# 24 weight tiles get their low half from an accumulating DMA instead of a GpSimd subtraction

## The chip, the cores and the metric

The kernel runs on one core of one Trainium2 chip. A core has five instruction queues that work side by side, each in its own order: TensorE (PE, matrix products; PEld is its weight load), VectorE (DVE), ScalarE (ACT), GpSimd (POOL) and SyncE (SP, which only issues DMAs). They wait for each other by semaphores. The time is device microseconds of one launch: median 2107.94 us of three runs (2106.41 to 2108.83).

## The reference

A residual stream of 256 tokens by 2048 channels in float32 goes through two layers, an S5 state-space mixer and windowed attention, each followed by a squared-ReLU MLP. The change lies in the gated unit at the end of the S5 mixer:

```python
    y = lax.map(per_example, ug).reshape(bsz, seq, dm)
    y = y + d_skip.astype(f32) * uf
    z = jax.nn.gelu(y).astype(u.dtype)
    return (z @ w_glu_a) * jax.nn.sigmoid(z @ w_glu_b)
```

`y` is the output of a bidirectional scan over time. Both weight matrices are 2048 by 2048 float32.

## The kernel before

**Products in three parts.** To get float32 accuracy, each weight tile is split into a high half in the format fp32r and a low half, raw minus high, also in fp32r. `mm3` (L686 to L688) makes each product in three matmuls: activation high times weight high (L686), activation low times weight high (L687), activation high times weight low (L688). So a tile's first two matmuls need only its high half, the third its low half.

**Preparing a tile.** `wload` takes the next tile from the list `self.wsrc`: it issues the load from HBM into a raw buffer (L662), casts it into the high half on ScalarE (L667) and subtracts into the low half (L668), on VectorE or, where the table `self.whow` says "g", on GpSimd. `wnext` calls `wload` ahead of use, one tile ahead as a rule. Buffers go round in rings that `wring` sets up: two raw buffers, three for high halves, three for low halves. For the early tiles of the gated unit two more raw buffers are lent (`wx`), until the eight output blocks of the second half begin and the third of them is done.

**The early gated unit.** Its weights come in 32 early tiles of 128 by 1024 (512 KB, `wge`), each loaded by a DMA that *ScalarE* issues, and 16 later tiles of 128 by 2048 (1 MB, `wgl`), loaded by SyncE. Each early tile feeds twelve matmuls of 128x512. The early tiles (`glu_early`, run by `glu` in `run`) depend only on the first half of `z`, so they are put between the pieces of the S5 mixer's second half: the scan on VectorE (L532 to L534), the expansion of the kernels on GpSimd (L550, L551) with their matmuls (L572) and copies out of PSUM (L590), and then eight output blocks, each with state copies (L608), matmuls (L636), every second one with a gelu (L641), a transposition (L648) and its split (L651, L652). Tiles 9 to 32 are the ones that the range `WP` marks (L1271): their subtraction is GpSimd's. Behind them come the 16 `wgl` tiles and then the MLP.

**What sets the order.** The program is written in one order and then rearranged by a scheduler at build time, so the order in each queue is what the listings of the instructions show. On the chip each queue keeps that order strictly: an instruction that waits holds back all that stand behind it on its engine, a DMA issue on ScalarE or GpSimd too.

Of the kernel before, what the change touches and what calls it, by code (L numbers as in the profile page):

```python
# [9 lines left out]
F32 = mybir.dt.float32  # L10
# [3 lines left out]
ALU = mybir.AluOpType  # L14
# [21 lines left out]
WP = range(9, 33)  # L36
# [131 lines left out]
class Kernel:  # L168
# [486 lines left out]
    def wload(self):  # L655
        if self.wsrc:
            src = self.wsrc.pop(0)
            if src is None:
                self.wring(D)
                src = self.wsrc.pop(0)  # L660
            raw, hi, lo = (r.next() for r in self.wr)
            (self.nc.scalar if raw.shape[1] < D else self.nc.sync).dma_start(raw, src)  # L662
            how = self.whow.get(len(self.wsrc), "v")
            m = raw.shape[1] // len(how)
            for i, e in enumerate(how):
                c = slice(i * m, (i + 1) * m)
                self.nc.scalar.copy(hi[:, c], raw[:, c])  # L667
                (self.nc.gpsimd if e == "g" else self.nc.vector).tensor_sub(lo[:, c], raw[:, c], hi[:, c].bitcast(F32))  # L668
            self.wq.append((hi, lo))

# [505 lines left out]
    def run(self):  # L1176
        nc, d, ar = self.nc, self.d, self.ar
# [8 lines left out]
        v, g = nc.vector, nc.gpsimd  # L1186
# [78 lines left out]
        def glu(n, m=GM):  # L1265
            for _ in range(n):
                next(ge, None)
                sc(m)

        n = len(self.wsrc)  # L1270
        self.whow.update({n - i: "g" for i in WP})  # L1271
        glu(GO)
        self.s5_ztrans(0, prev)
        ar.free("st0", "u0")
# [2 lines left out]
        raw = self.wr[0].tiles  # L1277
# [120 lines left out]
```

## Time and profile before

| | before |
|---|---|
| median of three runs | 2107.94 us |
| span of the profiled execution, first to last instruction | 2103.6 us |
| what the median has beyond that span | 4.3 us |
| instructions | 33054 |
| GpSimd busy in the whole span | 331.0 us |
| of it the subtractions L668 (all 36) | 101.1 us |
| wait of TensorE for L668 of GpSimd (matmuls) | 8.1 us in 5 waits, the longest 4.0 us |

The profile has a page of one execution: busy time per engine, the span in slices, the DMA queues, the chain that ended last, and groups of instructions by line. The trace behind it answers further: a timeline (start, duration, engine, line, operation, output and inputs, count, and in brackets the idle time before with what ended it), busy time per stretch of the span, and waits. "slot" stands for any piece of the big on-chip buffer, "bank" for PSUM. The span is what one execution's instructions cover; the runs' times contain a few microseconds more.

The profiled execution has no run time of its own on record beside its span, so the table sets the span beside the median of the runs.

### The profile page before, as it was taken

The page shows a single profiled execution, that of the slowest core. Times are in us where ns is not written, and L with a number is a line of the kernel's source. Part 1 is how long each engine was busy: PE and PEld are TensorE (multiplying, and loading weights), DVE is VectorE, ACT ScalarE, POOL GpSimd, SP SyncE. Part 2 cuts the span into 40 slices and gives each one's busy share as a digit, 9 for nine tenths or more (in the row PEclk, how much of TensorE's full clock was granted, in tenths as well). Part 3 has the DMA queues.
Part 4 walks back from the last instruction along what each step waited for, and adds up shares of the span by engine and source line. Part 5 has one row for each costly group of instructions (what it writes and reads, how often), then busy time and mean ns, then how long its engine had stood idle before and what let it go on. Part 6 is the DMA issues. An engine that isn't in the chain of part 4 may idle for free.

```text
span 2103.6 us, 33054 instructions
## 1 busy us (share of the span) xinstructions
PE 2030.6 (97%) x13844; PEld 1705.0 (81%) x13844; DVE 1245.0 (59%) x1824; ACT 974.7 (46%) x1238; POOL 331.0 (16%) x248
## 2 busy tenths in 40 slices
PE   4989999999999999999999889999999999999999
PEld 4877778788888888888887667888888888888887
DVE  8889736655555554444556877465555555444444
ACT  6553645444444444434434556554444444443442
POOL 6988721200000000000003330100000000000000
PEclk9999999999999999999999999999999999999999
DMA  3224455455555555655554332455555555555554
GB/s 120 73 93 144 152 199 196 154 200 188 193 180 184 193 184 200 213 188 199 202 186 153 115 128 96 146 185 200 188 193 186 195 184 196 200 187 193 200 187 153
DMA packets 59685, 364.28 MB, mean 173 GB/s; under 512 B 6816, under 2 KB 9152, under 8 KB 19600
## 3 DMA queue, kind: packets, MB, share of 16 engines
q1 hardware_dynamic: 54144, 342.32, 46.4%
q10 hardware_dynamic: 5184, 19.49, 2.8%
q8 instruction: 108, 1.77, 0.3%
q0 software_dynamic: 208, 0.36, 0.0%
q14 instruction: 41, 0.34, 0.0%
HBM read 360.05 MB, written 2.10 MB: 172 GB/s over the span
## 4 chain that ended last, share of the span: by engine, by line
PE 75%; DVE 4%; ACT 2%; DMA 1%; issue 1%; POOL 0%; SPq 0%; ACTq 0%; DVEq 0%
PE bank L878 33%; PE bank L827 23%; PE bank L828 11%; PE bank L686 2%; PE bank L687 2%; PE bank L688 2%; DVE slot L668 1%; ACT slot L667 1%; ACT slot L1039 1%; PE bank L1058 1%; DMA slot<-in_wqkv 1%; PE bank L1049 1%; DVE slot L1043 1%; DVE slot L1024 1%; DMA slot<-in_wup 0%
## 5 line engine op out<-in xcount | busy, mean ns | idle before, releaser
L668 DVE TENSOR_TENSOR slot<-slot,slot 128x2048 fp32r<-128x2048 f32 (+1 forms) x321 | 713.6, 2225 | 737.0 <-ACT slot L667 733.3
L667 ACT CAST slot<-slot 128x2048 fp32r<-128x2048 f32 (+2 forms) x357 | 623.5, 1752 | 743.0 <-PE bank L878 368.4
L827 PE MATMUL bank<-slot,slot 128*128 128x512 f32 x2048 | 720.0, 397 | 0.0
L878 PE MATMUL bank<-slot,slot 128*128 128x512 f32 x3072 | 696.7, 389 | 0.0
L878 PEld LDWEIGHTS bank<-slot,slot 128*128 128x128 f32 x3072 | 576.5, 188 | 119.6
L828 PE MATMUL bank<-slot,slot 128*128 128x256 f32 x2048 | 572.0, 280 | 0.0
L827 PEld LDWEIGHTS bank<-slot,slot 128*128 128x128 f32 x2048 | 385.5, 188 | 92.5
L828 PEld LDWEIGHTS bank<-slot,slot 128*128 128x128 f32 x2048 | 386.9, 189 | 0.3
L686 PE MATMUL bank<-slot,slot 128*128 128x512 f32 x544 | 217.3, 401 | 6.8 <-ACT slot L667 5.2
L688 PE MATMUL bank<-slot,slot 128*128 128x512 f32 x544 | 207.7, 395 | 8.3 <-POOL slot L668 8.1
L687 PE MATMUL bank<-slot,slot 128*128 128x512 f32 x544 | 213.6, 393 | 0.0
L686 PEld LDWEIGHTS bank<-slot,slot 128*128 128x128 f32 x544 | 102.7, 189 | 31.4 <-ACT slot L667 6.5
L836 ACT ACTIVATE slot<-slot 128x256 f32<-128x256 f32 x128 | 53.6, 420 | 160.4 <-DVE slot L835 160.4
L688 PEld LDWEIGHTS bank<-slot,slot 128*128 128x128 f32 x544 | 101.6, 188 | 32.0 <-POOL slot L668 10.1
L687 PEld LDWEIGHTS bank<-slot,slot 128*128 128x128 f32 x544 | 102.8, 189 | 20.4 <-issue 0.5
L668 POOL TENSOR_TENSOR slot<-slot,slot 128x1024 fp32r<-128x1024 f32 (+2 forms) x36 | 101.1, 2818 | 102.5 <-ACT slot L667 97.2
L949 POOL DMA_DIRECT2D slot<-in_pos x1 | 0.8, 754 | 613.1 <-DVE slot L871 613.1
L532 DVE TENSOR_TENSOR bank<-bank,slot 128x256 f32<-128x256 f32 x126 | 54.4, 431 | 4.1
L835 DVE SCALAR_TENSOR_TENSOR slot<-slot 128x256 f32<-128x256 f32 x128 | 54.2, 425 | 4.2
L704 POOL TENSOR_TENSOR slot<-slot 128x512 f32<-128x512 f32 x16 | 28.9, 1814 | 170.6 <-DVE slot L1157 61.5
L870 ACT CAST slot<-slot 128x256 fp32r<-128x256 f32 x128 | 51.0, 400 | 8.3 <-PE bank L878 8.3
L871 DVE TENSOR_TENSOR slot<-slot,slot 128x256 fp32r<-128x256 f32 x128 | 53.3, 419 | 1.7 <-ACT slot L870 1.6
(217 smaller groups left out, 1389.0 us busy)
## 6 DMA issues: line engine op xcount, KB each, us to landing
slot<-in_wup SPq DMA_DIRECT2D x128, 1024.0 KB, 4.8
slot<-in_wdn SPq DMA_DIRECT2D x128, 1024.0 KB, 4.8
slot<-in_wqkv SPq DMA_DIRECT2D x20, 1024.0 KB, 4.9
slot<-in_wge ACTq DMA_DIRECT2D x32, 512.0 KB, 3.7
slot<-in_wgl SPq DMA_DIRECT2D x16, 1024.0 KB, 5.3
slot<-in_wo SPq DMA_DIRECT2D x16, 1024.0 KB, 4.9
slot<-in_bz SPq DMA_DIRECT2D x16, 336.0 KB, 3.5
slot<-in_cp SPq DMA_DIRECT2D x16, 256.0 KB, 2.7
```

The lines of the kernel that those rows point to most:

```text
L532: yield v.tensor_mul(xy, lb, st[:, k - 1].rearrange("p r (o g) -> p r o g", o=1).broadcast_to([P, 2, 2, n]))
L667: self.nc.scalar.copy(hi[:, c], raw[:, c])
L668: (self.nc.gpsimd if e == "g" else self.nc.vector).tensor_sub(lo[:, c], raw[:, c], hi[:, c].bitcast(F32))
L686: pe.matmul(out, lhsT=xh, rhs=wh, start=first, stop=False)
L687: pe.matmul(out, lhsT=xl, rhs=wh, start=False, stop=False)
L688: pe.matmul(out, lhsT=xh, rhs=wl, start=False, stop=last)
L827: pe.matmul(bk, lhsT=wh[:, kt], rhs=act[:, kt].rearrange("p x c -> p (x c)"), start=(kt == 0), stop=False)
L828: pe.matmul(bk[:, :L], lhsT=wl[:, kt], rhs=act[:, kt, 0], start=False, stop=(kt == KT - 1))
L835: nc.vector.scalar_tensor_tensor(s, s, 0.0, rb, op0=ALU.max, op1=ALU.mult)
L836: nc.scalar.activation(hT(fb), s, AF.Square)
L871: nc.vector.tensor_sub(hl, hT(kt), hh.bitcast(F32))
L878: pe.matmul(bks[tt][cb], lhsT=x[:, ts], rhs=w[:, cb * 512:(cb + 1) * 512], start=(kt == 0 and w is wh and x is hh), stop=(kt == NK - 1 and ...
```

## The change

A new letter "d" in `self.whow` takes the place of "g" for tiles 9 to 32. For these the high half is made as before. Then ScalarE writes the raw tile times -1.0 into the low half, which rounds it to fp32r and so gives the negative of the high half, and GpSimd issues a DMA that adds the raw tile to it in float32. The low half is then raw minus high, as before.

```diff
@@ -665,6 +665,10 @@
             for i, e in enumerate(how):
                 c = slice(i * m, (i + 1) * m)
                 self.nc.scalar.copy(hi[:, c], raw[:, c])
+                if e == "d":
+                    self.nc.scalar.mul(lo[:, c], raw[:, c], -1.0)
+                    self.nc.gpsimd.dma_start(lo[:, c].bitcast(F32), raw[:, c], accum_op=ALU.add)
+                    continue
                 (self.nc.gpsimd if e == "g" else self.nc.vector).tensor_sub(lo[:, c], raw[:, c], hi[:, c].bitcast(F32))
             self.wq.append((hi, lo))
 
@@ -1268,7 +1272,7 @@
                 sc(m)
 
         n = len(self.wsrc)
-        self.whow.update({n - i: "g" for i in WP})
+        self.whow.update({n - i: "d" for i in WP})
         glu(GO)
         self.s5_ztrans(0, prev)
         ar.free("st0", "u0")
```

The lines of the changed kernel behind L668 have numbers that are four higher (L590 and L550 keep theirs). The scaling is its L669, the accumulating DMA its L670.

GpSimd's queue, where the first of these tiles stand. slot_2734 and slot_2733 hold high and low halves, slot_241 and slot_81 raw tiles, the others the kernel expansion; in brackets are the semaphores that a row waits for. Before:

```order
L551 TENSOR_TENSOR slot_313<-slot_313,slot_79 128x8x64 [waits Pool_49]
L668 TENSOR_TENSOR slot_2734<-slot_241,slot_2734 128x1024 [waits DVE_49,DMAHW1_49,PE_49,Activation_49]
L550 TENSOR_TENSOR slot_79<-slot_83 128x512 [waits Pool_49]
L668 TENSOR_TENSOR slot_2734<-slot_241,slot_2733 128x1024 [waits DVE_49,DMAHW3_49,PE_49,Activation_49]
L551 TENSOR_TENSOR slot_313<-slot_313,slot_79 128x8x64 [waits Pool_49]
L668 TENSOR_TENSOR slot_2734<-slot_81,slot_2733 128x1024 [waits DVE_49,DMAHW5_49,PE_49,Activation_49]
```

And in the changed kernel:

```order
L551 TENSOR_TENSOR slot_313<-slot_313,slot_79 128x8x64 [waits Pool_49]
L550 TENSOR_TENSOR slot_79<-slot_83 128x512 [waits Pool_49]
L670 DMA slot_2734<-slot_241 128x1024 [waits DMAHW1_49,Activation_49]
L551 TENSOR_TENSOR slot_313<-slot_313,slot_79 128x8x64 [waits Pool_49]
L670 DMA slot_2734<-slot_241 128x1024 [waits DMAHW3_49,Activation_49]
L550 TENSOR_TENSOR slot_79<-slot_83,slot_73 128x512 [waits Pool_49]
L551 TENSOR_TENSOR slot_313<-slot_313,slot_79 128x8x64 [waits Pool_49]
L550 TENSOR_TENSOR slot_79<-slot_83,slot_73 128x512 [waits Pool_49]
L670 DMA slot_2734<-slot_81 128x1024 [waits DMAHW5_49,PE_49,Activation_49]
```

These are tiles 9, 10 and 11. One more piece of the expansion (L550) now stands ahead of tile 9's low half, and three more (L550, L551, L550) ahead of tile 11's.

ScalarE's queue, tiles 14 to 18. Here a load (L662) refills a raw buffer. Before, it waited for the subtraction that last read that buffer (Pool):

```order
L662 DMA slot_241<-in_wge 128x1024 [waits Pool_49]
L667 CAST slot_2733<-slot_81 128x1024 [waits DMAHW5_49,PE_49]
L662 DMA slot_81<-in_wge 128x1024 [waits DMAHW0_49,Pool_49]
L667 CAST slot_2733<-slot_241 128x1024 [waits DMAHW6_49,PE_49]
L662 DMA slot_81<-in_wge 128x1024 [waits Pool_49]
L590 COPY slot_83<-bank 128x512 [waits PE_49]
L662 DMA slot_241<-in_wge 128x1024 [waits Pool_49]
L667 CAST slot_2734<-slot_241 128x1024 [waits DMAHW7_49,PE_49]
```

In the changed kernel it waits for the landing of the accumulate that last read it. DMASW0 to DMASW7 are the eight completion semaphores of GpSimd's DMAs in turn, beginning with tile 9, so DMASW5 is tile 14's, DMASW0 here tile 17's:

```order
L662 DMA slot_241<-in_wge 128x1024 [waits DMASW5_49,Activation_49]
L667 CAST slot_2734<-slot_81 128x1024 [waits DMAHW4_49,PE_49]
L669 ACTIVATE slot_2734<-slot_81 128x1024 [waits PE_49]
L667 CAST slot_2733<-slot_81 128x1024 [waits DMAHW5_49,PE_49]
L669 ACTIVATE slot_2734<-slot_81 128x1024 [waits PE_49]
L667 CAST slot_2733<-slot_241 128x1024 [waits DMAHW6_49,PE_49]
L669 ACTIVATE slot_2734<-slot_241 128x1024 [waits PE_49]
L662 DMA slot_81<-in_wge 128x1024 [waits DMAHW0_49,DMASW6_49,Activation_49]
L662 DMA slot_81<-in_wge 128x1024 [waits DMASW7_49,Activation_49]
L590 COPY slot_83<-bank 128x512 [waits PE_49]
L662 DMA slot_241<-in_wge 128x1024 [waits DMASW0_49,Activation_49]
L667 CAST slot_2734<-slot_241 128x1024 [waits DMAHW7_49,PE_49]
```

The casts of tiles 15, 16 and 17 stand behind the load that waits for tile 14's accumulate, the cast of tile 18 behind the one that waits for tile 17's; before, loads and casts alternated.

ScalarE's queue, where the last loads stand. The changed kernel:

```order
L662 DMA slot_241<-in_wge 128x1024 [waits DMASW3_49,Activation_49]
L1309 DMA slot_73<-in_xt 128x4096 [waits PE_49]
L667 CAST slot_2734<-slot_241 128x1024 [waits DMAHW4_49,PE_49]
L669 ACTIVATE slot_2734<-slot_241 128x1024 [waits PE_49]
L651 CAST slot_3776<-bank 128x2x256 [waits PE_49]
L641 ACTIVATE slot_73<-bank 128x8x4x16 [waits PE_49,Activation_49]
L651 CAST slot_3776<-bank 128x2x256 [waits PE_49]
L662 DMA slot_241<-in_wge 128x1024 [waits DMASW4_49,Activation_49]
L662 DMA slot_241<-in_wge 128x1024 [waits DMASW5_49,Activation_49]
```

The 2 MB of the residual stream (`in_xt`) are issued ahead of the loads of tiles 31 and 32, as before. But before, the load of tile 31 came right behind them and that of tile 32 ahead of the last split (L651); now both stand behind it and wait for the accumulates of tiles 29 and 30.

## The prediction

> **What bounds the kernel now.** The page comes first: TensorE is busy 97% of the span, so the other engines only matter where they make it wait. The change touches the 24 tiles numbered 9 to 32 of the early gated unit. GpSimd's rows put them between 200 and 294 us, so I cut that part of the span into three stretches, with the one behind it. The columns are busy us (and count) of PE, PEld, DVE, ACT and POOL, the granted clock, DMA share and GB/s; the number after the stretch is its length.
>
> ```profile
> PE 2030.6 (97%) x13844; PEld 1705.0 (81%) x13844; DVE 1245.0 (59%) x1824; ACT 974.7 (46%) x1238; POOL 331.0 (16%) x248
> 197.00:203.00 6.00, 1.80 (x25) 0.85 (x14) 5.42 (x18) 0.37 (x1) 6.00 (x5) 1.00 0.22 61
> 203.00:287.00 84.00, 83.73 (x941) 67.40 (x941) 53.31 (x104) 49.78 (x59) 56.49 (x27) 0.98 0.54 181
> 287.00:296.00 9.00, 6.86 (x28) 4.79 (x27) 0.50 (x1) 4.53 (x4) 4.74 (x2) 1.00 0.03 11
> 300.00:350.00 50.00, 50.00 (x226) 41.38 (x225) 31.53 (x24) 25.59 (x23) 4.35 (x3) 1.00 0.62 228
> ```
>
> From 203 to 287 us TensorE has no gap worth naming. Whatever GpSimd is spared there is worth nothing, and whatever makes TensorE wait there is lost in full. Behind 300 us TensorE is full again on work that follows from the last tile, so a delay at the end of the tiles passes to the end of the program one to one. The only time to be won lies at the two ends, and the first one is GpSimd's:
>
> ```profile
> 197.90 0.40 PE L687 MATMUL bank<-slot,slot 128*128 128x512 f32 x1
> 202.28 0.50 PE L688 MATMUL bank<-slot,slot 128*128 128x512 f32 x1 [3.98 <-POOL slot L668]
> ...
> 206.00 0.63 PE L686 MATMUL bank<-slot,slot 128*128 128x512 f32 x1
> 206.42 0.44 PE L687 MATMUL bank<-slot,slot 128*128 128x512 f32 x1
> 206.70 0.40 PE L688 MATMUL bank<-slot,slot 128*128 128x512 f32 x1
> 206.93 0.39 PE L686 MATMUL bank<-slot,slot 128*128 128x512 f32 x1
> ```
>
> TensorE waits 3.98 us for tile 9's low half, and after it starts a matmul only every 0.43 us (206.00 to 206.42) until the step is 0.23 us again (206.70 to 206.93). GpSimd's timeline says why it was late, and when each low half was ready (start plus duration):
>
> ```profile
> 196.53 2.17 POOL L550 TENSOR_TENSOR slot<-slot,slot 128x512 f32<-128x512 f32 x2 [1.72 <-DMA slot<-in_cp]
> 198.66 1.27 POOL L551 TENSOR_TENSOR slot<-slot,slot 128x512 f32<-128x512 f32 x1
> 199.88 2.35 POOL L668 TENSOR_TENSOR slot<-slot,slot 128x1024 fp32r<-128x1024 f32 x1
> 202.18 1.11 POOL L550 TENSOR_TENSOR slot<-slot 128x512 f32<-128x512 f32 x1
> ...
> 218.65 9.49 POOL L668 TENSOR_TENSOR slot<-slot,slot 128x1024 fp32r<-128x1024 f32 x4
> 229.81 2.42 POOL L668 TENSOR_TENSOR slot<-slot,slot 128x1024 fp32r<-128x1024 f32 x1 [1.68 <-ACT slot L667]
> ...
> 236.60 7.50 POOL L668 TENSOR_TENSOR slot<-slot,slot 128x1024 fp32r<-128x1024 f32 x3 [1.65 <-ACT slot L667]
> ...
> 254.13 2.38 POOL L668 TENSOR_TENSOR slot<-slot,slot 128x1024 fp32r<-128x1024 f32 x1 [1.64 <-ACT slot L667]
> ...
> 265.01 2.41 POOL L668 TENSOR_TENSOR slot<-slot,slot 128x1024 fp32r<-128x1024 f32 x1 [3.54 <-ACT slot L667]
> ...
> 273.25 2.39 POOL L668 TENSOR_TENSOR slot<-slot,slot 128x1024 fp32r<-128x1024 f32 x1 [1.80 <-ACT slot L667]
> ...
> 288.79 4.74 POOL L668 TENSOR_TENSOR slot<-slot,slot 128x1024 fp32r<-128x1024 f32 x2 [8.47 <-ACT slot L667]
> ```
>
> In tile numbers: 9 is ready at 202.2, 14 at 221.0 and 17 at 228.1 (the four from 218.65), 18 at 232.2, 20 at 239.1 and 22 at 244.1 (first and last of the three from 236.60), 25 at 256.5, 27 at 267.4, 29 at 275.6, 31 at 291.2, 32 at 293.5.
>
> **The change, part by part.** *Removed:* 24 subtractions on GpSimd. *Added:* 24 scalings on ScalarE and 24 accumulating DMAs, issued by GpSimd.
>
> ```profile
> L668 POOL TENSOR_TENSOR slot<-slot,slot 128x1024 fp32r<-128x1024 f32 x24 | 57.6, 2409 | 29.2 <-ACT slot L667 24.0 <-PE bank L636 4.7 <-PE bank L688 0.6
> L667 ACT CAST slot<-slot 128x1024 fp32r<-128x1024 f32 x24 | 24.9, 1050 | 28.2 <-PE bank L687 12.3 <-POOL slot L668 6.2 <-DVE slot L533 5.4
> L608 ACT COPY slot<-slot 64x504 f32<-64x504 f32 x16 | 18.1, 1130 | 3.5 <-PE bank L636 3.2
> L608 DVE COPY slot<-slot 64x504 f32<-64x504 f32 x16 | 22.1, 1384 | 11.4 <-PE bank L636 11.1
> L836 ACT ACTIVATE slot<-slot 128x256 f32<-128x256 f32 x128 | 53.6, 420 | 160.4 <-DVE slot L835 160.4
> L870 ACT CAST slot<-slot 128x256 fp32r<-128x256 f32 x128 | 51.0, 400 | 8.3 <-PE bank L878 8.3
> L949 POOL DMA_DIRECT2D slot<-in_pos x1: 754/754/754, 1010.9 to 1010.9; - x1
> L949 POOL DMA_DIRECT2D slot<-in_band x1: 538/538/538, 1021.8 to 1021.8; - x1
> ```
>
> GpSimd loses 57.6 us of work and gets 24 issues of 0.54 to 0.75 us, 13 to 18 us; it is no limit any more. ScalarE gets a scaling of a 128x1024 tile, which no row of before shows. The cast of that tile takes 1.05 us, and where the trace has both kinds on one shape an activation costs 5% more (420 ns against 400), so 1.05 to 1.10; below the cast I expect nothing, as the instruction comes on top. I take the cast's 1.05: 25 us more on an engine that is busy 49.8 of 84 us. That would fit, were it not for order.
>
> The price that decides is **T, from the issue of an accumulate on GpSimd to its landing.** No accumulate stands in the trace. The nearest rows (last number: us from issue to landing):
>
> ```profile
> slot<-in_wup SPq DMA_DIRECT2D x128, 1024.0 KB, 4.8
> slot<-in_wge ACTq DMA_DIRECT2D x32, 512.0 KB, 3.7
> slot<-in_cp SPq DMA_DIRECT2D x16, 256.0 KB, 2.7
> slot<-in_bca SPq DMA_DIRECT2D x16, 128.0 KB, 2.0
> slot<-in_xt ACTq DMA_DIRECT2D x1, 2048.0 KB, 12.2
> slot<-in_band POOLq DMA_DIRECT2D x1, 256.0 KB, 4.9
> slot<-in_pos POOLq DMA_DIRECT2D x1, 1.0 KB, 4.7
> ```
>
> Through GpSimd's queue 256 KB took 4.9 us where other queues took 2.7; going from 256 to 512 KB costs 1.0 (3.7 - 2.7), so a plain 512 KB from GpSimd would take 5.9. An accumulate also reads its destination, 512 KB more: 1.1 us (4.8 - 3.7). **T = 7.0 us** is my value. As ends I keep 2.0 (the shortest landing in these rows) and 12.2 (the longest, a transfer that shares the queues). The subtraction it replaces took 2.41.
>
> The raw buffer and the low half are held until T is over. And the load that refills a raw buffer is an instruction *in ScalarE's queue*, which waits for that landing with the next casts standing behind it. Before, it waited for a subtraction 2.4 us long. So the landings come one after another. From the order of ScalarE's and GpSimd's instructions in the changed kernel, with R(n) the time at which tile n's low half is ready:
>
> - R(9): GpSimd's four pieces of kernel expansion now stand ahead of the issue (196.53 + 2.17 + 1.27 + 1.11, so 201.1): 201.1 + T, against 202.2.
> - 9 to 14: TensorE finishes tile 9 at the slow cadence (ten matmuls at about 0.4, 4.0 us) and tile 10 (twelve at 0.23, 2.7), which frees high halves; then cast and scaling of 13 and 14 (4.2): 10.9 + T, against 18.8.
> - 14 to 17: the load waits for 14 ahead of casts 15, 16, 17; six ScalarE instructions (6.1 with their hand-over) and the issue, 0.34: 6.5 + T, against 7.1.
> - 17 to 18, and 18 to 20: load, cast, scaling: 2.5 + T each, against 4.1 and 6.9.
> - 20 to 22: load and scaling: 1.5 + T, against 5.0.
> - 22 to 25: load, scaling of 24, two copies and a gelu (1.13, 1.13, 0.6), cast, scaling: 6.3 + T, against 12.4.
> - from 25 on there are two raw buffers: 25 to 27 is a load from HBM (3.7), a cast, a copy out of PSUM, a scaling: 6.4 + T, against 10.9. 27 to 29: 5.8 + T against 8.2. 29 to 31: 5.8 + T against 15.5, which was so long because the load of 31 ran right behind the 2 MB of `xt`; it is now issued later.
> - 31 to 32: 2.1, against 2.3, its cast and scaling.
>
> Where the new step is shorter than the old, I keep the old: TensorE has that much work in it. Only in 29 to 31 it idles, 2.1 us between 287 and 296 (9.00 - 6.86), and so much that step can shrink. With T = 7: +5.9 at tile 9, then 0, 6.4, 5.4, 2.6, 3.5, 0.9, 2.5, 4.6, -2.1, 0: **+30 us at tile 32.** The span becomes 2133. The span of before was 2103.6 and the median of the runs 2107.9; I take the 4.3 between them as unchanged: **2138 us.**
>
> Costed at nothing: TensorE's order (a dozen matmuls trade places, all in the list above), VectorE's copies, which no longer share time with subtractions, and the bytes. The 24 accumulates write 12.6 MB and read it twice; DMA share is 0.54 in the stretch. If that cover fails, loads land later, and T takes it up in the same places. A scaling of 1.10 us would add 0.05 in some 14 places, 0.7 us.
>
> The pages on the chip speak to T. By the Trainium skill, "DMA: Bandwidth & Descriptors", section "Anatomy of one DMA — SWDGE (gpsimd) path", a GpSimd DMA takes about 2.0 us plus its bytes at 436 GB/s, which by that page is an estimated 3.2 us for this one; in the list above that gives about +5 us, not +30. The trace speaks against its fixed part: 1 KB took 4.7 us here. By the Trainium skill, "SBUF — State Buffer", section "Who interferes with whom", a VectorE copy in its two-port mode shuts GpSimd out, descriptor writing included; the 16 VectorE copies of 1.38 us between 233 and 273 us could then lengthen T. No row of before shows either at an accumulate.
>
> **The rivals.**
> - *Quick landing, T between 3.0 and 4.5.* For it: both ends of the transfer are in SBUF, and no HBM is read. Against: even 1 KB took 4.7 us through GpSimd's queue. At T = 3.7 the start (2.6), 14 to 17 (3.1), 17 to 18 (2.1), 20 to 22 (0.2) and 27 to 29 (1.3) cost, less the 2.1 us at the end: +7, 2115. At 4.5: +11, 2119. Chance 0.14.
> - *Slow landing, T of 9 or more*: reading two streams and adding them may run far below a plain copy, and three accumulates can be in flight at once. For it: the 12.2 us row. At T = 10 the steps from 9 to 31 give 2.1 + 9.4 + 8.4 + 5.6 + 6.5 + 3.9 + 5.5 + 7.6 + 0.3, with 8.9 at the start: +58, 2166. At 12.2: +80, 2188. Chance 0.24.
> - *Not slower*: the accumulate is ready about when the subtraction was. At T = 1.1 tile 9 is ready at 202.2 as before, only 14 to 17 costs anything (0.5), and the 2.1 us at the end are won: 2106. It decides at T = 1.9, where start, 14 to 17 and 17 to 18 cost the 2.1 us; up to T = 3.0 the loss stays within 4 us. Against it stands each row of GpSimd's queue. Chance 0.06.
>
> **How the numbers follow.** Forecast (T between 4.5 and 9, 2119 to 2156) 0.56, quick 0.14, slow 0.24, not slower 0.06. Range 2115 (T = 3.7) to 2172 (T = 10.6): it leaves out half of the quick, the slowest of the slow and the not slower, some 0.2 together. A measurement of this kernel can tell 0.2% (4 us) from no change: slower 0.94, within 0.2% 0.05, faster 0.01.
>
> **What would show it.** In the changed trace: GpSimd's 24 DMA issues of about 0.6 us and 7 us to landing; ScalarE's casts waiting for a DMA of GpSimd's queue or standing behind a load that does; TensorE's wait at 198.3 grown from 4 to about 10 us; low-half matmuls waiting for DMA in the stretch that had no gap; the first `wgl` cast near 323 instead of 293.6 us; nothing changed behind it but the shift. I am wrong if the landing is near 3 us, if TensorE has no new gaps between 203 and 287, or if the time behind 300 us takes part of the delay back.

## The result, and the profile after

The changed kernel takes 2144.33 us (median of 4 runs, 2140.78 to 2151.56), the kernel before 2107.19 us beside it (2106.41 to 2108.83). The ratio is **1.018, 95% interval 1.0163 to 1.0197: 1.8% slower, clear of the noise.** The profiled executions have spans of 2140.4 and 2103.6 us, 36.8 us apart.

The page of the changed kernel: busy time of the engines, two of the DMA queues (packets, MB, share of 16 engines' span), and the group of low-half matmuls (busy us, mean ns, idle us before them and what ended most of it).

```profile
PE 2044.4 (96%) x13844; PEld 1713.5 (80%) x13844; DVE 1232.1 (58%) x1824; ACT 996.3 (47%) x1262; POOL 295.2 (14%) x248
q0 software_dynamic: 3664, 12.95, 3.2%
q10 hardware_dynamic: 5184, 19.49, 2.7%
L692 PE MATMUL bank<-slot,slot 128*128 128x512 f32 x544 | 211.4, 405 | 33.5 <-DMA slot<-slot 30.6
```

The same number of matmuls, and a new wait: 30.6 us for DMAs from SBUF to SBUF, which are the accumulates (queue q0). GpSimd lost 35.8 us of work (331.0 to 295.2), and nobody gained by it. Where the time went shows in the stretches of the trace (columns as in the prediction). The changed kernel:

```profile
203.00:287.00 84.00, 69.80 (x770) 53.30 (x771) 37.84 (x101) 49.25 (x56) 20.36 (x22) 0.93 0.92 219
287.00:332.00 45.00, 30.69 (x199) 23.21 (x196) 3.30 (x5) 19.51 (x23) 5.16 (x6) 0.83 0.79 210
340.00:2140.00 1800.00, 1773.52 (x9048) 1488.18 (x9046) 1006.65 (x1274) 814.04 (x990) 104.36 (x55) 0.99 0.51 181
```

and the kernel before, behind the same work:

```profile
302.00:2103.00 1801.00, 1772.56 (x9047) 1487.42 (x9046) 1007.15 (x1274) 813.76 (x990) 104.32 (x55) 1.00 0.51 181
```

The stretch from 203 to 287 us, which had 83.73 us of TensorE in 84.00, has 69.80; DMA share went from 0.54 to 0.92. Behind the tiles 1800 us hold what 1801 held: nothing is won back there and nothing more is lost. The whole loss lies between tile 9 and tile 32, about half of it behind 287 us: the 45 us from 287 to 332, with the last six tiles, hold 30.69 of TensorE. The end of the program shifts with it. The first `wgl` cast, which follows the last tile, stands at 331.68 us, 38.1 later than at 293.56.

The first gap, on TensorE of the changed kernel:

```profile
198.28 0.40 PE L691 MATMUL bank<-slot,slot 128*128 128x512 f32 x1
206.18 0.80 PE L692 MATMUL bank<-slot,slot 128*128 128x512 f32 x1 [7.50 <-DMA slot<-slot]
...
207.20 0.63 PE L691 MATMUL bank<-slot,slot 128*128 128x512 f32 x1
207.63 0.63 PE L692 MATMUL bank<-slot,slot 128*128 128x512 f32 x1
...
211.20 0.39 PE L692 MATMUL bank<-slot,slot 128*128 128x512 f32 x1
211.42 0.40 PE L690 MATMUL bank<-slot,slot 128*128 128x512 f32 x1
```

The wait of 3.98 us has become 7.50 and its releaser is a DMA; behind it stands the same slow cadence as before, 0.43 us from matmul to matmul (207.20 to 207.63), until it is 0.22 again (211.20 to 211.42).

T, from an accumulate's issue to its landing, is read from three views: GpSimd's issues (L670), ScalarE's loads (L662), each of which starts when the accumulate it waits for has landed, and the summary of the line. GpSimd's issues of tiles 14, 17, 18, 27, 28 and 29:

```profile
219.69 0.86 POOL L670 DMA_DIRECT2D slot<-slot  x1 [1.02 <-ACT slot L669]
...
235.02 0.94 POOL L670 DMA_DIRECT2D slot<-slot  x1 [1.04 <-ACT slot L669]
246.55 0.86 POOL L670 DMA_DIRECT2D slot<-slot  x1 [10.59 <-ACT slot L669]
...
290.05 0.86 POOL L670 DMA_DIRECT2D slot<-slot  x1 [10.23 <-ACT slot L669]
294.13 0.86 POOL L670 DMA_DIRECT2D slot<-slot  x1 [3.22 <-ACT slot L669]
308.17 0.86 POOL L670 DMA_DIRECT2D slot<-slot  x1 [13.18 <-ACT slot L669]
```

The summary of that line over its 24 issues:

```profile
DMA to landing us min/median/max: 4.5/6.2/11.5
```

ScalarE's loads that the same landings release, with what comes between the last of them:

```profile
228.50 0.33 ACTq L662 DMA_DIRECT2D slot<-in_wge  x1
...
243.82 0.33 ACTq L662 DMA_DIRECT2D slot<-in_wge  x1
244.25 1.05 ACT L667 CAST slot<-slot 128x1024 fp32r<-128x1024 f32 x1 [4.47 <-DMA slot<-slot]
...
251.18 0.33 ACTq L662 DMA_DIRECT2D slot<-in_wge  x1
...
295.38 0.33 ACTq L662 DMA_DIRECT2D slot<-in_wge  x1
...
305.87 1.05 ACT L667 CAST slot<-slot 128x1024 fp32r<-128x1024 f32 x1 [7.47 <-DMA slot<-in_wge]
305.98 0.33 ACTq L662 DMA_DIRECT2D slot<-in_wge  x1
...
318.23 2.83 ACTq L662 DMA_DIRECT2D slot<-in_wge  x2
```

Tile 14: 228.50 - 219.69 = 8.8 us. Tile 17: 243.82 - 235.02 = 8.8. Tile 18, with no other accumulate in flight: 251.18 - 246.55 = 4.6. Read in this way for every tile on which the prediction's steps stand (times "ready" in us; the column for before and the predicted shift follow from the prediction):

| tile | ready before | predicted shift | ready after | measured shift | T |
|---|---|---|---|---|---|
| 9 | 202.2 | +5.9 | 206.2 | +4.0 | 5.0 |
| 14 | 221.0 | +5.9 | 228.5 | +7.5 | 8.8 |
| 17 | 228.1 | +12.3 | 243.8 | +15.7 | 8.8 |
| 18 | 232.2 | +17.7 | 251.2 | +19.0 | 4.6 |
| 22 | 244.1 | +23.8 | 268.5 | +24.4 | 6.4 |
| 25 | 256.5 | +24.7 | 282.3 | +25.8 | 7.5 |
| 27 | 267.4 | +27.2 | 295.4 | +28.0 | 5.3 |
| 29 | 275.6 | +31.8 | 318.2 | +42.6 | 10.1 |
| 32 | 293.5 | +29.7 | 331.7 | +38.2 | 5.1 |

Up to tile 27 the shift is the predicted one within 3.4 us. Then one step, 27 to 29, costs 10 us more than was said: 22.8 us (295.4 to 318.2) where 12.8 was predicted. From 29 to 32 the shift shrinks by 4.4, where 2.1 was predicted.

### The profile page after: what moved, and what is told of

The parts are those of the page before. It is cut to its first block, busy times and chain, and to the rows that moved or that the text cites. A ratio compares the mean times of both kernels' runs of the same rounds, so it can differ in the third digit from the quotient of the medians.

```text
span 2140.4 us, 33091 instructions
## 1 busy us (share of the span) xinstructions
PE 2044.4 (96%) x13844; PEld 1713.5 (80%) x13844; DVE 1232.1 (58%) x1824; ACT 996.3 (47%) x1262; POOL 295.2 (14%) x248
## 4 chain that ended last, share of the span: by engine, by line
PE 74%; DVE 4%; ACT 2%; DMA 1%; issue 1%; POOL 0%; SPq 0%; ACTq 0%; DVEq 0%
PE bank L882 32%; PE bank L831 22%; PE bank L832 11%; PE bank L690 2%; PE bank L691 2%; PE bank L692 2%; DVE slot L672 1%; ACT slot L1043 1%; ACT slot L667 1%; PE bank L1062 1%; PE bank L1053 1%; DMA slot<-in_wqkv 1%; DMA slot<-in_wup 0%; DVE slot L1028 0%; DVE slot L1047 0%
## 5 line engine op out<-in xcount | busy, mean ns | idle before, releaser
L692 PE MATMUL bank<-slot,slot 128*128 128x512 f32 x544 | 211.4, 405 | 33.5 <-DMA slot<-slot 30.6
L672 POOL TENSOR_TENSOR slot<-slot,slot 128x2048 fp32r<-128x2048 f32 (+1 forms) x12 | 43.7, 3653 | 73.9 <-ACT slot L667 73.9
L838 DVE TENSOR_TENSOR slot<-bank,slot 128x256 f32<-128x256 f32 x128 | 53.4, 417 | 0.4 <-ACT slot L840 0.2
```

Of the source, the lines that this page charges most:

```text
L692: pe.matmul(out, lhsT=xh, rhs=wl, start=False, stop=last)
L838: nc.vector.tensor_add(s, bk[:, :L], t)
```

## The experiments

Two theories stood against each other. **Serial:** the landings come one after another, because the loads wait for them in ScalarE's queue; what counts is T. **Engines:** the DMA engines are full (share 0.92), and what counts is their time. A third question was what the scaling costs. Where nothing else is said, all 24 tiles are edited. "Cast" is the first `wgl` cast, as a shift against 293.56 us; T is the median of a run's line. A cast belongs to the one profiled execution, and it contains what that execution was late ahead of tile 9. The last `in_cp` load shows how much: 192.27 us in the kernel before, 0.1 to 0.4 later in the changed kernel and with the scaling alone, the first nine tiles or one tile, 0.7 to 1.3 later with the loads on SyncE, the dummies and the subtractions on VectorE, but 2.5 to 3.1 later with the plain copy, both 64 KB kernels and the last fifteen tiles. So casts differ by that much without the tiles.

**The scaling alone.** The subtraction stays on GpSimd, and ScalarE's scaling is done ahead of it (tiles 9 to 32 get the letter "s").

```diff
+                if e == "s":
+                    self.nc.scalar.mul(lo[:, c], raw[:, c], -1.0)
-                (self.nc.gpsimd if e == "g" else self.nc.vector).tensor_sub(lo[:, c], raw[:, c], hi[:, c].bitcast(F32))
+                (self.nc.gpsimd if e in "gs" else self.nc.vector).tensor_sub(lo[:, c], raw[:, c], hi[:, c].bitcast(F32))
```

> The kernel before, with ScalarE's 24 scalings added (raw times -1.0 into the low half) and GpSimd's subtractions kept, which then overwrite the low half: the scalings alone. Theory of serial landings (the loss comes from loads in ScalarE's queue that wait for accumulates, with casts behind them): each tile is ready 1.05 us later and nothing else, so 0 to 4 us over the kernel before. Rival, ScalarE's own work (25 us more on a queue that also carries the state copies): 12 us or more, up to 25.

Measured: 2112.74 us, ratio 1.0024 (1.0008 to 1.0039); cast at 297.55, +4.0. So the scalings, costed at nothing beside their place in the steps, cost 4 us by the cast and 6 by the medians (2106.51 for the kernel before beside it), a tenth to a sixth of the loss.

**A plain copy in place of the accumulate.** This leaves out the subtraction of the high half.

```diff
-                    self.nc.gpsimd.dma_start(lo[:, c].bitcast(F32), raw[:, c], accum_op=ALU.add)
+                    self.nc.gpsimd.dma_start(lo[:, c].bitcast(F32), raw[:, c])
```

> The changed kernel, with a plain copy of the raw tile into the low half in place of the accumulating one (leaves out the subtraction of the high half). Theory of serial landings with T made of a queue part and the second read: T falls from 6.2 us by about 1, the loss of 37 us by about 10. Rival, the DMA engines' time (an accumulate takes 2.85 us of all 16 engines, a load of the same size 1.55): their share in the stretch falls from 0.89 to 0.99 to about 0.75, loads land in 3.8 instead of 4.6 us, and the loss falls by 15 us or more.

Measured: 2122.29 us, ratio 1.0067 (1.0041 to 1.0094); cast +17.6. Its page has, for the queue and the issues (last number: median us to landing):

```profile
q0 software_dynamic: 3664, 12.95, 1.6%
slot<-slot POOLq DMA_DIRECT2D x24, 512.0 KB, 3.9
```

The plain copy lands in 3.9 us where the accumulate takes 6.2, in as many packets and bytes. By q0's share it takes 1.6% of 2119.4 us = 34 us of 16 engines, 1.4 us each; the accumulates take 3.2% of 2140.4 = 68 us, 2.85 us each. The adding doubles the engines' time and adds 2.3 us to T.

**The loads in another queue.** In the changed kernel, the `in_wge` loads are issued by SyncE, so that no cast stands behind a load that waits.

```diff
-            (self.nc.scalar if raw.shape[1] < D else self.nc.sync).dma_start(raw, src)
+            self.nc.sync.dma_start(raw, src)
```

> The changed kernel, with the early tiles' loads issued by SyncE instead of ScalarE, so that no cast stands behind a load that waits for an accumulate; the accumulates and their bytes stay. Theory of serial landings: the steps 14 to 17, 17 to 18, 18 to 20 and 20 to 22 fall back to what three high-half buffers allow, 8 to 15 us less than the changed kernel (2129 to 2136). Rival, the DMA engines' time: the same bytes through the same engines, within 3 us of the changed kernel.

Measured: 2137.33 us, ratio 1.0136 (1.0116 to 1.0156); cast +34.0; 7 us less than the changed kernel by the medians, 4 by the casts. Neither theory's number: the queue's order is a part, and 30 of the 37 us stay without it. That the engines are then the limit is one reading; the other is that each load still waits for a landing, now in SyncE's queue. This run doesn't tell them apart. The stretches of this kernel, DMA share next to last:

```profile
205.00:250.00 45.00, 42.10 (x443) 32.36 (x444) 29.11 (x84) 24.90 (x29) 13.38 (x15) 0.89 1.02 245
250.00:285.00 35.00, 32.92 (x385) 25.49 (x383) 7.99 (x13) 28.15 (x32) 5.54 (x6) 1.00 0.87 223
```

Share 1.02, and T has grown to 6.9 us.

**Engine time alone.** To the kernel before, ScalarE's queue gives 24 transfers of 1 MB from HBM to HBM, one behind each of the casts; nobody waits for them, and the subtractions are GpSimd's again (the declaration of `dum` is left out here).

```diff
-                self.nc.scalar.copy(hi[:, c], raw[:, c])
+                cast = self.nc.scalar.copy(hi[:, c], raw[:, c])
...
+                if e == "g" and raw.shape[1] < D:
+                    k = self.ndum = getattr(self, "ndum", -1) + 1
+                    with self.tc.issue_after(cast.ins):
+                        self.nc.scalar.dma_start(self.d["dum"][k], self.d["wdn"][1, k])
```

> The kernel before, with 24 additional transfers of 1 MB from HBM to an unused place in HBM, issued by ScalarE right behind the casts of tiles 9 to 32; nothing waits for their data. About the engine time of the accumulates (1 MB of load costs about 3 us of all 16 engines) without their waits. Theory of serial landings: GpSimd still subtracts, loads land 1 us later, so less than 6 us over the kernel before. Rival, the DMA engines' time: 15 us or more over it.

Measured: 2127.65 us, ratio 1.0089 (1.006 to 1.0117); cast +18.7. The dummies take the engines about as long as the accumulates did (2.65 us each by q10's share, 5.7% against 2.7%), with share 1.00, 0.86 and 1.01 in the stretches here:

```profile
205.00:250.00 45.00, 42.02 (x465) 32.34 (x465) 30.90 (x87) 20.32 (x24) 34.28 (x17) 0.97 1.00 383
250.00:285.00 35.00, 35.00 (x452) 28.67 (x449) 16.95 (x16) 26.96 (x31) 16.21 (x7) 1.00 0.86 319
285.00:300.00 15.00, 6.03 (x19) 4.20 (x18) 0.00 (x0) 1.61 (x2) 3.63 (x2) 0.66 1.01 388
```

TensorE stays full from 250 to 285 us at that share and loses 9 of 15 us behind it, where late loads reach it. So 24 transfers that nobody waits for cost something like half of the loss without an accumulate, most of it behind 285 us, where about half of the change's own loss lies. Whether that is the engines' time alone stays open: the dummies stand in the same DMA queue (q10) as the `in_wge` loads, whose median landing went from 3.7 to 5.8 us on the page, and a load can have stood behind a dummy there.

**Serial landings without the bytes.** The accumulate covers 128 of 1024 columns, 64 KB; in a second kernel, SyncE then copies the same 64 KB once more behind it (the last line, which only the second has). Both leave out the subtraction for the other columns, and the second undoes it for these.

```diff
-                    self.nc.gpsimd.dma_start(lo[:, c].bitcast(F32), raw[:, c], accum_op=ALU.add)
+                    q = slice(i * m, i * m + 128)
+                    self.nc.gpsimd.dma_start(lo[:, q].bitcast(F32), raw[:, q], accum_op=ALU.add)
+                    self.nc.sync.dma_start(lo[:, q].bitcast(F32), raw[:, q])
```

> The changed kernel, with the accumulate over the first 128 of each tile's 1024 columns only (64 KB; leaves out the subtraction for the other columns): all scalings, waits and issues stay, an eighth of the bytes moves. T should be about 3.5 us. Theory of serial landings: the steps of the prediction with T = 3.5 give +6, with the 5 us that the scalings alone cost +6 to +11. Rival, the DMA engines' time: nothing but the scalings is left, +3 to +6.

> As x10_small, and behind each small accumulate a plain copy of the same 64 KB by SyncE's queue, which waits for its landing (leaves out the subtraction as before): the time from a GpSimd issue to a usable low half is about 6 us as in the changed kernel, with the DMA engines nearly idle. Theory of serial landings: the steps with T = 6 give +21 (2127), at least +15. Rival, the DMA engines' time: within 4 us of x10_small.

Measured: the first 2122.74 us, ratio 1.0084 (1.0067 to 1.0102), cast +14.8; the second 2133.48 us, ratio 1.0143 (1.0111 to 1.0174), cast +30.3. The issues of the second:

```profile
slot<-slot POOLq DMA_DIRECT2D x24, 64.0 KB, 2.9
slot<-slot SPq DMA_DIRECT2D x24, 64.0 KB, 1.8
```

Two landings in a row (2.9 + 1.8, some 4.7 us) instead of one (2.9) cost 15.5 us more by the casts and 10.7 by the medians. The mean DMA share is nearly the same in both, 0.58 and 0.62 from 205 to 250 us, and 0.55 and 0.51 from 250 to 285, so the engines' time doesn't explain it: **a longer landing costs time with hardly a byte more.** How much per us is less clear. ScalarE's loads that the landings of tiles 27 and 30 release, in the first kernel:

```profile
279.71 0.33 ACTq L662 DMA_DIRECT2D slot<-in_wge  x1
...
298.49 0.36 ACTq L662 DMA_DIRECT2D slot<-in_wge  x1
```

and in the second:

```profile
286.06 0.33 ACTq L662 DMA_DIRECT2D slot<-in_wge  x1
...
313.72 0.33 ACTq L662 DMA_DIRECT2D slot<-in_wge  x1
```

At tile 27 the second is 6.4 us behind the first (286.06 - 279.71), and the prediction's list gives 7.1 for landings of 4.7 against 2.9: the serial theory's number, though not step by step, since at tile 17 the second was 0.8 ahead. The other nine come between tiles 27 and 30. There the DMA share is 0.8 in both (285 to 300 us), and the second kernel's copies stand in SyncE's queue with an `in_wgl` load (290.68) and the gains (291.31), the next copy only at 300.71. So 15.5 us is not the price of 1.8 us of landing alone. Put in a row by landing time, 2.9, 3.9, 4.7 and 6.2 us, the shifts are 14.8, 17.6, 30.3 and 38.1: they rise with it, but not evenly.

**Which tiles.** The change for tiles 9 to 17 alone, and, with `i >= 18` in the same line, for tiles 18 to 32 alone.

```diff
+        self.whow.update({n - i: "d" if i < 18 else "g" for i in WP})
```

> The changed kernel with the accumulate for tiles 9 to 17 only; tiles 18 to 32 are subtracted on GpSimd as before. By the steps of the prediction with T = 7: +5.9 at tile 9, 0, 6.4 for 14 to 17, and half of 17 to 18: +12 to +17. Rival (one stretch alone does it, the one with two raw buffers): under +6.

> The changed kernel with the accumulate for tiles 18 to 32 only. By the steps with T = 7: 18 to 20 2.6, 20 to 22 3.5, 22 to 25 0.9, 25 to 27 2.5, 27 to 29 4.6, less 2.1, and 5.4 for 17 to 18: +12 to +18; with the loads as late as they were in the changed kernel (27 to 29 took 22.9 us there) up to +25. Rival (the loss sits at the start): under +6.

Measured: 2117.61 us, ratio 1.0065 (1.0043 to 1.0088), cast +11.8; and 2129.6 us, ratio 1.0116 (1.0099 to 1.0133), cast +25.0. By the medians the two cost 12.3 and 24.3 us over the kernel before beside them (2105.3), 36.6 together, and the whole change 37.1: the parts add, as steps of a chain would. By the prediction's list with the measured T (5.8 and 5.4), the first nine should cost 9.9, and the rest, with the step from 17 to 18 (3.8), 8.5. The first is nearly right; the second is some 16 short by both measures, so most of what the list lacks is behind tile 17.

The summary of the DMA's line (min, median, max of T) in the kernel with the last fifteen:

```profile
DMA to landing us min/median/max: 4.6/5.4/11.4
```

in the one with the plain copy:

```profile
DMA to landing us min/median/max: 2.8/3.9/11.0
```

and in the one with a single landing of 64 KB:

```profile
DMA to landing us min/median/max: 2.3/2.9/7.9
```

One landing in each is far out. In the last of them it is that of tile 28, as the timelines of GpSimd, SyncE and ScalarE show there:

```profile
281.12 0.86 POOL L671 DMA_DIRECT2D slot<-slot  x1 [2.96 <-ACT slot L669]
...
281.49 1.01 SPq L702 DMA_DIRECT2D slot<-in_gains  x2
...
289.11 0.34 ACTq L662 DMA_DIRECT2D slot<-in_wge  x1
289.54 1.05 ACT L667 CAST slot<-slot 128x1024 fp32r<-128x1024 f32 x1 [5.62 <-DMA slot<-slot]
```

Even 64 KB took 7.9 us there (281.12 to 289.0), beside a 1 MB `in_wgl` load (280.99) and the two gains loads that SyncE issues, and the load of tile 29 on ScalarE's queue (279.71). SyncE's timeline of the changed kernel has the same company at its place:

```profile
291.55 0.33 SPq L662 DMA_DIRECT2D slot<-in_wgl  x1
292.51 1.36 SPq L701 DMA_DIRECT2D slot<-in_gains  x2
```

and in the rows of the changed kernel above, tile 28's accumulate (294.13) lands just ahead of the load that starts at 305.98, with the largest T, 11.5 us, while the load of tile 29, issued at 295.38, ends its cast's wait 10.5 us later (305.87). Before, that load was issued at 267.45, ahead of `in_wgl` at 273.14: the landing it now waits for has put it behind. This is the missing part of the step 27 to 29. That SyncE's loads are what delays it is read from their company, and the kernel with the loads on SyncE limits it. In GpSimd's, TensorE's and SyncE's timelines there, tile 28's accumulate, its low half's first matmul, and the gains:

```profile
288.04 0.86 POOL L670 DMA_DIRECT2D slot<-slot  x1 [3.20 <-ACT slot L669]
...
296.81 0.50 PE L692 MATMUL bank<-slot,slot 128*128 128x512 f32 x1 [3.51 <-DMA slot<-slot]
...
297.84 0.92 SPq L701 DMA_DIRECT2D slot<-in_gains  x2
```

The longest landing, 11.2 us, is again the one beside the gains: tile 29's, issued at 297.91. But tile 28's took about 8.8 (288.04 to 296.81) before `in_wgl` (297.20) and the gains were issued. So these transfers are not the whole cause; what else delays tile 28 stays open.

**One accumulate alone.** Tile 24 only.

```diff
+        self.whow.update({n - i: "d" if i == 24 else "g" for i in WP})
```

> The kernel before, with the scaling and the accumulate for tile 24 alone; the other 23 subtractions stay on GpSimd. One accumulate, with no other beside it. If T (issue to landing of an accumulate) is 6.2 us because of what the transfer itself is (two reads and a write, 512 KB each), this one lands in 5.5 to 6.5 us. If T is made by the company of other accumulates and of loads on full DMA engines (share 0.9 to 1.0 in the changed kernel against 0.5 here), it lands in 4.0 to 4.8, near the 3.9 of the plain copy and the shortest accumulate of the changed kernel (4.5). The issue on GpSimd 0.86 us by both. Its 16 engines' time 2.85 us if that is the work itself, below 2.2 if contention stretched it. The time: 0 to 4 us more than before by both.

```profile
slot<-slot POOLq DMA_DIRECT2D x1, 512.0 KB, 4.8
```

T is 4.8 us, at the end of the range for company: of the 6.2 us, about 1.4 seems to be made by other accumulates and full engines (one transfer against a median), and the table shows how: 4.6 and 5.3 for one with no other accumulate in flight, 8.8 for the last of two or three issued 1.9 us apart, when each takes 2.85 us of the engines. The engines' time of one transfer is too small to be read from a share of the span. Its one time, 2115.85 us, is 9 above the median of before, while the cast is 1.4 later; the rest lies behind 300 us, and 17 runs of before beside it went from 2101.73 to 2113.25, so one run says nothing of it.

**The late subtractions on VectorE.** From the kernel before, and without scaling or accumulate, tiles 9, 31 and 32 are subtracted by VectorE; in a second kernel, with `(9, 10, 11, 12, 31, 32)` in the same line, those six.

```diff
-        self.whow.update({n - i: "g" for i in WP})
+        self.whow.update({n - i: "g" for i in WP if i not in (9, 31, 32)})
```

> The kernel before, with the low halves of tiles 9, 31 and 32 subtracted by VectorE and the other 21 by GpSimd as before; no scaling, no accumulate. My theory: a tile's low half counts by when it is ready, and tile 9's was late only because it stood in GpSimd's queue behind the kernel expansion (199.88 + 2.35 us, while its cast was over by 194). VectorE subtracts this shape in 1.3 us, so TensorE's 3.98 us wait at 198.3 goes, and the half cadence behind it with it; tiles 31 and 32 are each ready about 1 us earlier, in a stretch where TensorE idles 2.1 us. First wgl cast at 287 to 290 us (293.6 in the kernel before), the time 4 to 6 us less than before, ratio 0.997 to 0.998. Rival, VectorE is the limit there: it is busy 5.42 of 6.00 us between 197 and 203, on a chain with TensorE's score matmuls, so 1.3 us more on it delays that chain, and the wait only changes its name: first wgl cast within 1 us of 293.6, ratio 1.000. Second rival, GpSimd's tile 10 is now the late one (its subtraction ends at about 205.6 as before): gain under 2 us.

> The kernel before, with the low halves of tiles 9 to 12, 31 and 32 subtracted by VectorE, the other 18 by GpSimd; no scaling, no accumulate. With 9, 31 and 32 alone on VectorE the wait moved from tile 9 (3.98 us) to tile 10 (3.50 us, GpSimd's queue) and the first wgl cast came 1.0 us earlier. My theory: what is late there is GpSimd's queue, not a tile, so the wait goes only when the subtractions beside the kernel expansion leave that queue together: TensorE's wait at 198 to 207 us falls below 1.5 us, the first wgl cast comes at 288 to 290 us (292.6 with three tiles, 293.6 before), ratio 0.997 to 0.998. Rival: VectorE, busy 13.73 of 15.00 us between 190 and 205, cannot take four more subtractions (5 us) without delaying the score matmuls it feeds: the wait stays at 3 us or more under another name, first wgl cast 292 or later, ratio 0.999 to 1.001.

TensorE's largest waits between 190 and 340 us (total us, times, longest), in the first:

```profile
PE bank L688 <- POOL slot L668: 3.5, 1, 3.5
```

and in the second:

```profile
PE bank L686 <- ACT slot L667: 2.0, 1, 2.0
...
PE bank L688 <- POOL slot L668: 0.7, 1, 0.7
```

With three tiles the wait went from tile 9 to tile 10, still in GpSimd's queue, and the cast came 1.0 us earlier: the second rival. With six the wait on GpSimd is down to 0.7 us, and the cast stands at 290.28, 3.3 us earlier, just short of the 288 to 290 expected. The times don't resolve it: 2105.59 us, ratio 0.9996 (0.9982 to 1.001), and 2104.45 us, ratio 0.9997 (0.9983 to 1.0011). 3.3 us are 0.16% of this kernel, inside both intervals. No version here is shown to beat the kernel before.

## Why the prediction was right, and where it was not

The forecast was 2138 us with slower at 0.94; 2144.33 lies 6 above it, inside the range. By its own steps:

- **What bounds it: right.** TensorE's stretch without a gap lost 13.9 us (83.73 to 69.80) to late tiles, and behind the tiles nothing came back: 1773.52 us busy in 1800 against 1772.56 in 1801. GpSimd's 35.8 spared us bought nothing.
- **The chain of landings: right, and shown for a part of the loss.** The 64 KB pair shows that a longer landing costs time at nearly the same DMA share (10.7 us by the medians, 6.4 at tile 27 where the list gives 7.1), and up to tile 27 the list's shifts hold within 3.4 us. Part of that closeness is luck: the start cost 4.0 and not 5.9, 9 to 14 was put at nothing and cost 3.5, and 17 to 18 cost 3.3 and not 5.4. That the chain runs *through ScalarE's loads* holds for a small part only: with the loads on SyncE, 30 of the 37 us stayed.
- **T = 7.0: nearly right as a whole, by parts that were wrong.** The median is 6.2 and the mean over the eleven landings on the chain 6.5 (the nine of the table, 20 at 5.7 and 31 at 4.5). But the plain 512 KB copy out of GpSimd's queue took 3.9 us, not 5.9: the rows for loads from HBM through that queue were no measure for SBUF to SBUF. The adding cost 2.3 in all, not 1.1: about 0.9 with no other accumulate beside it (4.8 against the plain copy's 3.9) and about 1.4 of company, which was not in the sum. The first error, 2.0 too much, and the second, 1.2 too little, nearly cancelled, which is luck.
- **The start: mis-sized by T.** A wait of "about 10 us" was 7.50, since tile 9's accumulate, the first in flight, took 5.0.
- **27 to 29: the step that failed.** 5.8 + T supposed a load from HBM at 3.7 us and a T like the others. The load took 10.5 and tile 29's accumulate 10.1, in the company of tile 28's accumulate, of 1 MB and 2 times 256 KB from SyncE, then of the 2 MB of `in_xt`; which of them delays it most is not tried apart. The prediction had seen that a load behind the residual stream is late (it explains the 15.5 us of 29 to 31 by it), and asked only who escapes that collision, not who now runs into one.
- **The scaling: 1056 ns as predicted, but not free.** Alone it costs 4.0 us by the cast; the list had it only where it stands between two landings. At T = 2.9 the list gives +3.8 and the run has +14.8; of the 11 between them 2.6 stand ahead of tile 9, and the scalings' 4.0 and 4.2 us that the run loses beyond the list behind tile 27 account for most of the rest. That T = 7.0 gives 6 us more than 6.2 would (29.7 against 23.3 in the list) hid part of this: with the measured T the list is 15 us short of the 38.2, and the forecast came within 6 us by a T that was too long.
- **Full engines: put at nothing.** The DMA share went from 0.54 to 0.92, the `in_wge` loads' median landing from 3.7 to 4.6 us on the page, and the dummies show that such traffic alone can cost 18.7 us (cast). How much of the change's own loss it makes is not shown.
- **GpSimd's issues:** 0.86 us each, where 0.54 to 0.75 was taken; it was no limit.
- **The rivals.** Quick landing fell (no T below 4.5), and not slower with it (by the list its break-even is T = 1.8, not 1.9). Slow landing came true for single tiles, 28 and 29, not for the median. By the Trainium skill, "DMA: Bandwidth & Descriptors", section "Anatomy of one DMA — SWDGE (gpsimd) path", the transfer was an estimated 3.2 us. The plain copy, 3.9, comes near it; the accumulate, 4.8 alone and 6.2 in company, does not. The VectorE copies that could shut GpSimd out (the Trainium skill, "SBUF — State Buffer", section "Who interferes with whom") left a small mark. Behind tile 10 all issues took 0.86 or 0.87 us but two, 0.94 (235.02) and 1.17 (262.09), and both ran beside VectorE's copies (L608), as VectorE's and GpSimd's timelines show for the second:

```profile
261.96 1.21 DVE L608 COPY slot<-slot 64x504 f32<-64x504 f32 x2 [24.82 <-PE bank L636]
262.09 1.17 POOL L670 DMA_DIRECT2D slot<-slot  x1 [5.42 <-ACT slot L669]
```

Not every issue beside such a copy is longer (0.86 at 254.70 in the second 64 KB kernel), and 0.4 us in two of 24 issues are no part of the 37.

## What to carry to other kernels

A DMA that takes an engine's place is a wait for whoever needs its result or its buffer next: find the instructions that will wait for the landing, and what stands behind them in that in-order queue, and count the landings in a row before the bytes. A landing time read from one kind of transfer holds for that kind and that company only; for every transfer that is moved later, ask beside which others it will now run. An engine that is relieved off the critical path gives nothing, and one that is late at a single place (here GpSimd at tile 9) passes its wait to the next item in its queue when only that one is taken away.

## What the runs showed of the hardware that was not expected

- An accumulating DMA from SBUF to SBUF takes twice the engine time of a plain one of the same bytes and packets: 2.85 against 1.4 us of 16 engines for 512 KB. Its issue takes GpSimd 0.86 us against 0.53.
- A GpSimd DMA of 64 KB within SBUF, accumulate and all, landed in 2.9 us, less than the 4.7 us of 1 KB from HBM in the prediction's rows.
- A small transfer is not small in company: 64 KB took 7.9 us beside 1.5 MB of loads on SyncE's queue and 512 KB on ScalarE's, where the run's median is 2.9.
